# Chain steps moved among the weight units of a two-block transformer kernel

## The chip, the cores and the metric

The kernel runs on one core of a Trainium2 chip. The metric is the device time of one execution in microseconds (us); less is better. TensorE (PE) multiplies matrices, and its weight loads (PEld) are listed apart; VectorE (DVE), ScalarE (ACT) and GpSimd (POOL) work element by element; SyncE (SP) issues the DMAs. Each engine works through its own instructions in a fixed order, and an instruction that waits holds up all that stand behind it on that engine.

## The reference

One sequence of 256 tokens with 1024 features goes through two blocks, all in float32. The first block has two layers; the second block one.

```
# first block, twice:
h = rms_norm(x); z = h @ w_in
cq, ckv, kpe, gq, gk, gv, glr, gr, su, gates = split(z)
o_a = mla_mixer(cq, ckv, kpe)   # low-rank attention: q = norm(cq) @ w_uq, k,v = norm(ckv) @ w_ukv
o_b = gla_mixer(gq, gk, gv)     # gated linear attention in chunks of 64
o_c = s5_mixer(su)              # diagonal state space scan, then a GLU
g = sigmoid(gates)              # three gates of 1024
x = x + (g0*(o_a @ w_br_mla) + g1*(o_b @ w_br_gla) + g2*(o_c @ w_br_s5)) @ w_out
x = x + square(relu(rms_norm(x) @ w_ff1)) @ w_ff2
# second block, once:
h = rms_norm(x); q, k, v, glu_in, z_ga, z_gc = split(h @ w_in_2)
y_attn = dilated_attention(q, k, v)                  # 3 groups of 8 heads of 64
u = a * sigmoid(gate), from glu_in                   # 1024 channels
y_conv = silu(layer_norm(depthwise_conv31(u))) @ w_conv_out
x = x + norm((sigmoid(z_ga)*y_attn + sigmoid(z_gc)*y_conv) @ w_mix_out)
x = x + norm((silu(h2 @ gate) * (h2 @ up)) @ w_ffn_out)   # h2 = rms_norm(x)
```

## The kernel before

**Products.** A float32 product is made of three float32r products: each operand is split into a high part H and a low part L, and H·H, L·H and H·L add up in PSUM. `mm_f` (lines 170 to 172) makes 128 output features by 256 tokens, eight blocks of 128 in the contraction, so 24 matmuls of 256 columns for one unit; `mm_t` (lines 176 to 178) makes 128 tokens by up to 512 features.

**Weight units.** The weights stream through the chip once. A unit is 128 rows by 1024 columns: a DMA on SP brings it into `raw`, ACT rounds it to `wH` (line 161), DVE subtracts to get `wL` (line 162), and 24 matmuls use it. Up to three units are prepared ahead. Behind its matmuls most units have an evacuation: ACT or DVE reads the PSUM tile and writes it to SBUF. The tiles `mm` for these have two buffers, so PE can't begin the third unit before the first is evacuated; the chains use `acc` (five buffers) and `tr` (one).

**Chains.** The attention, state space, linear attention and convolution parts are written as generators, one `yield` at each place where they must wait for another engine. They are the chains: `s` (S5, `s5_run`), `l` (gated linear attention, `gla`), `t` (the row statistics of the latents), `a` and `b` (the two halves of the heads in `mla_attn`); and in the second block `c` (depthwise convolution, `conv_gen`), `h` (heads of the dilated attention, `heads`), `n` (layer norm behind the convolution) and `b` (bias tables).

**Order.** Three strings set the order: `SCHED[0]` and `SCHED[1]` for the two layers and `SCHED2` for the second block. A token with a number is a weight unit (`g1_2` is the third unit of gate 1, `ukv1` the unit that makes keys and values of the second half of the heads, `b2_1` the product of branch 2 with its output weights, `co` the convolution's output, `zc` and `za` gates of the second block, `A` and `G` the two halves of the GLU, `m` the mixing product); a token of one letter is one step of that chain, and `!s` runs chain `s` to its end. The functions are called in this order; a scheduler then orders the instructions of each engine, mostly by that order.

**Lines that the prediction speaks of.** In `mla_kv_evac` ACT squares the keys (`mla_sq`, line 852), DVE and POOL make their norms, DVE writes `mla_kn` (lines 861, 862), and ACT then copies the values to `mla_v` (line 863). In `mla_attn` a step `turn_qk` transposes `mla_qn` and `mla_kn` on PE (line 881), `scores` multiplies them (lines 894, 895), and a later step transposes the probabilities (line 919) and multiplies by the values (line 930). The gates' evacuation is `gt` (line 1116). In S5 one step multiplies by `ET` (line 558), the next runs the scan and writes `s5z` (line 578), the next multiplies by it (lines 587, 591). In the linear attention line 699 multiplies `gq` and `gk`, and lines 739 and 745 make its outputs. In the second block the softmax of a head pair is at lines 1487 and 1491 on ACT, its transposes at line 1500 on PE, copied to `pT` (line 1504); the convolution's layer norm ends with a silu (line 1429), and `cH`, `cL` are its split output for the units `co` (lines 1620, 1621).

Of the kernel before, what the change touches and what calls it, by code (L numbers as in the profile page):

```python
# [13 lines left out]
AF = mybir.ActivationFunctionType  # L14
OP = mybir.AluOpType
# [3 lines left out]
S = 256  # L19
# [48 lines left out]
def f_blocks(w, l, c0, nk, n=1):  # L68
    return [(w, l, k, c0 + P * j, c0 + P * (j + 1)) for j in range(n) for k in range(nk)]
# [201 lines left out]
def residual_raw(k, t, accs, scale, g, dst):  # L271

    nc = k.nc
    with k.tc.high_priority(PRI_N):
        for h in range(2):
# [769 lines left out]
def f_unit(k, plan, st, blocks, evac, nk=8):  # L1045
    def run(H, L):
        ps = k.mm_tile()
        k.mm_f(ps[:, :S], H, L, st.hH, st.hL, nk)
        with k.tc.high_priority(PRI_E):
            evac(ps)  # L1050
    plan.unit(blocks, run)
# [481 lines left out]
def plan_second(k, plan, st):  # L1533
    nc = k.nc
    Q0, K0, V0, A0, G0, ZA, ZC = 0, 1536, 3072, 4608, 5632, 6656, 7680
    st.v2, st.q, st.k, st.u = {}, {}, {}, {}

    def gains(u):
        return [k.pp("gpre")[:, i:i + 1] for i in (2 * u, 2 * u + 1)]
# [14 lines left out]

    def glu_a(i):
        def evac(ps):
            st.ga = k.t1("ga")
            nc.scalar.activation(st.ga, ps[:, :S], AF.Identity, bias=k.pp("bglua")[:, i:i + 1])
        f_unit(k, plan, st, f_blocks("w_in_2", 0, A0 + i * P, 8), evac)

    def glu_gate(i):
        def evac(ps):
            th = k.t1("g2th")
            nc.scalar.activation(th, ps[:, :S], AF.Tanh, scale=0.5, bias=k.pp("bglug")[:, i:i + 1])
            u = k.main.tile([P, 30 + S], F32, tag="u", name=f"u{i}")
            nc.vector.memset(u[:, 0:30], 0.0)
            nc.vector.scalar_tensor_tensor(u[:, 30:30 + S], th, 1.0, st.ga, op0=OP.add, op1=OP.mult)
            st.u[i] = u
        f_unit(k, plan, st, f_blocks("w_in_2", 0, G0 + i * P, 8), evac)

# [18 lines left out]
    za, zc, mm, m1, box = {}, {}, {}, {}, {}  # L1589
# [63 lines left out]
    for tok in SCHED2.split():  # L1653
        name, n = tok.rstrip("0123456789"), tok[len(tok.rstrip("0123456789")):]
# [112 lines left out]
CONV_A = (3, 7, 11, 15, 19, 23, 27)  # L1767
NT = "mtmt"
AT1 = 1
PRI_N = 30  # L1770
PRI_M = 30
AT = 1
SCHED = (
# [8 lines left out]
)  # L1782
SCHED2 = (
# [5 lines left out]
)  # L1789
HOLD = 3  # L1790
RAW_V = 1
# [4 lines left out]
def build_plan(k, tc, ins, out, dbg=None):  # L1796
    plan = make(k, tc, ins, out, dbg)
    k.ins, k.out = ins, out
    sts = [K(), K(), K()]
    plan.do(lambda: first(k, sts[0]))  # L1800
    plan_layer(k, plan, 0, sts[0], sts[1], 3)
    plan_layer(k, plan, 1, sts[1], sts[2], 4)
    plan_second(k, plan, sts[2])
    return plan
# [253 lines left out]
class None_TC:  # L2058
    nc = None
# [38 lines left out]
```

## Time and profile before

| | us |
|---|---|
| median of 3 runs | 1443.59 (1443.32 to 1445.24) |
| the profiled execution | 1446.86 |
| its span, first to last instruction | 1445.1 |
| PE busy | 1403.0 (97%) |
| PE weight loads busy | 1274.8 (88%) |
| DVE busy | 1012.7 (70%) |
| ACT busy | 832.2 (58%) |
| POOL busy | 48.5 (3%) |
| DMA | 243.10 MB, mean 168 GB/s |

All times are one execution's. A stretch is named by its start and end in us from the first instruction. Layer 0 takes about 0 to 530 us, layer 1 to about 950, and the second block the rest; the two layers' feed-forward parts and the one of the second block come at the end of each. "PEclk" is the granted clock of PE as a share of 2.4 GHz, so 0.50 is 1.2 GHz.

### The profile page before, as it was taken

The page shows a single profiled execution, that of the slowest core. Times are in us where ns is not written, and L with a number is a line of the kernel's source. Part 1 is how long each engine was busy: PE and PEld are TensorE (multiplying, and loading weights), DVE is VectorE, ACT ScalarE, POOL GpSimd, SP SyncE. Part 2 cuts the span into 40 slices and gives each one's busy share as a digit, 9 for nine tenths or more (in the row PEclk, how much of TensorE's full clock was granted, in tenths as well). Part 3 has the DMA queues.
Part 4 walks back from the last instruction along what each step waited for, and adds up shares of the span by engine and source line. Part 5 has one row for each costly group of instructions (what it writes and reads, how often), then busy time and mean ns, then how long its engine had stood idle before and what let it go on. Part 6 is the DMA issues. An engine that isn't in the chain of part 4 may idle for free.

```text
span 1445.1 us, 26152 instructions
## 1 busy us (share of the span) xinstructions
PE 1403.0 (97%) x10412; PEld 1274.8 (88%) x10412; DVE 1012.7 (70%) x1860; ACT 832.2 (58%) x1455; POOL 48.5 (3%) x51
## 2 busy tenths in 40 slices
PE   7999999999999999999999999999999999999998
PEld 6989898989889889888998999989888979789997
DVE  6967776689455658676667555579999956765555
ACT  6865475467754555465546444466568574644443
POOL 1000111000000000021000000000000000000000
PEclk9999999999999999999999999999999999999999
DMA  6621444555455552334456555565555435465553
GB/s 221 219 88 62 144 153 140 177 192 189 160 173 187 201 179 78 114 121 173 158 178 227 187 186 189 189 215 190 184 159 164 172 133 198 143 213 190 188 185 109
DMA packets 71058, 243.10 MB, mean 168 GB/s; under 512 B 7864, under 2 KB 11656, under 8 KB 70936
## 3 DMA queue, kind: packets, MB, share of 16 engines
q1 hardware_dynamic: 70936, 241.43, 49.4%
q8 instruction: 81, 1.33, 0.4%
q14 instruction: 41, 0.34, 0.1%
HBM read 237.17 MB, written 4.23 MB: 167 GB/s over the span
## 4 chain that ended last, share of the span: by engine, by line
PE 67%; DVE 11%; ACT 5%; DMA 2%; issue 2%; POOL 2%; DVEq 0%; POOLq 0%; SPq 0%; ACTq 0%
PE mm L170 12%; PE mm L171 12%; PE mm L172 12%; PE acc L176 8%; PE acc L177 8%; PE acc L178 8%; DVE wL L162 3%; DMA raw<-in_wst_dram 2%; DVE cv L1372 2%; POOL rsq L185 2%; ACT wH L161 2%; ACT sp L1487 1%; PE acc L558 1%; ACT sp L1491 1%; PE acc L895 0%
## 5 line engine op out<-in xcount | busy, mean ns | idle before, releaser
L162 DVE TENSOR_TENSOR wL<-raw,wH 128x1024 fp32r<-128x1024 f32 (+1 forms) x410 | 495.8, 1210 | 260.3 <-ACT wH L161 254.7
L161 ACT ACTIVATE wH<-raw 128x1024 fp32r<-128x1024 f32 (+1 forms) x410 | 429.1, 1048 | 388.3 <-PE mm L171 204.5
L170 PE MATMUL mm<-hH,wH 128*128 128x256 f32 x1792 | 515.2, 287 | 5.7 <-ACT gt L1116 4.0
L171 PE MATMUL mm<-hL,wH 128*128 128x256 f32 x1792 | 510.8, 285 | 0.0
L172 PE MATMUL mm<-hH,wL 128*128 128x256 f32 x1792 | 510.7, 285 | 0.0
L170 PEld LDWEIGHTS mm<-hH,wH 128*128 128x128 f32 x1792 | 344.5, 192 | 18.0 <-issue 4.8
L171 PEld LDWEIGHTS mm<-hL,wH 128*128 128x128 f32 x1792 | 344.8, 192 | 4.1 <-issue 0.9
L172 PEld LDWEIGHTS mm<-hH,wL 128*128 128x128 f32 x1792 | 344.8, 192 | 1.0 <-issue 0.6
L176 PE MATMUL acc<-wH,fH 128*128 128x512 f32 x344 | 135.4, 394 | 0.0
L178 PE MATMUL acc<-wH,fL 128*128 128x512 f32 x344 | 134.3, 390 | 0.6 <-DVE fL L162 0.6
L177 PE MATMUL acc<-wL,fH 128*128 128x512 f32 x344 | 134.8, 392 | 0.0
L178 PEld LDWEIGHTS acc<-wH,fL 128*128 128x128 f32 x344 | 64.6, 188 | 15.4 <-DVE fL L162 1.3
L1372 DVE SCALAR_TENSOR_TENSOR cv<-u,ppt,cv 128x256 f32<-128x256 f32 x184 | 77.9, 478 | 0.4
L176 PEld LDWEIGHTS acc<-wH,fH 128*128 128x128 f32 x344 | 64.9, 189 | 11.9 <-ACT fH L161 0.7
L177 PEld LDWEIGHTS acc<-wL,fH 128*128 128x128 f32 x344 | 64.9, 189 | 10.5
L161 ACT ACTIVATE fH<-ffr 128x256 fp32r<-128x256 f32 x56 | 23.4, 418 | 66.8 <-DVE ffr L1275 66.6
L162 DVE TENSOR_TENSOR fL<-ffr,fH 128x256 fp32r<-128x256 f32 x56 | 23.7, 423 | 23.5 <-ACT fH L161 23.5
L178 PE MATMUL acc<-wH,hL 128*128 128x512 f32 x96 | 37.9, 394 | 0.9 <-DVE hL L165 0.8
L176 PE MATMUL acc<-wH,hH 128*128 128x512 f32 x96 | 38.2, 399 | 0.5 <-ACT hH L164 0.4
L177 PE MATMUL acc<-wL,hH 128*128 128x512 f32 x96 | 37.8, 394 | 0.9 <-DVE wL L162 0.9
L177 PE MATMUL acc<-wL,mH 128*128 128x512 f32 x96 | 37.8, 394 | 0.0
L176 PE MATMUL acc<-wH,mH 128*128 128x512 f32 x96 | 37.8, 394 | 0.0
(445 smaller groups left out, 2165.9 us busy)
## 6 DMA issues: line engine op xcount, KB each, us to landing
raw<-in_wst_dram SPq DMA_DIRECT2D x420, 512.0 KB, 3.4
xd<-x SPq DMA_DIRECT2D x6, 512.0 KB, 3.5
x<-xd SPq DMA_DIRECT2D x6, 512.0 KB, 4.6
bias<-bdram SPq DMA_DIRECT2D x8, 384.0 KB, 6.5
gnorm<-in_rows_dram SPq DMA_DIRECT2D x3, 512.0 KB, 5.5
raw<-in_wst_dram SPq DMA_DIRECT2D x4, 384.0 KB, 3.5
x<-in_x_dram SPq DMA_DIRECT2D x4, 256.0 KB, 4.2
x<-in_x_dram SPq DMA_DIRECT2D x2, 512.0 KB, 5.8
```

The lines of the kernel that those rows point to most:

```text
L161: nc.scalar.activation(H, src, AF.Copy)
L162: nc.vector.tensor_sub(L, src, H)
L170: nc.tensor.matmul(ps, H[:, w], aH[:, i, :], start=(i == 0), stop=False)
L171: nc.tensor.matmul(ps, H[:, w], aL[:, i, :], start=False, stop=False)
L172: nc.tensor.matmul(ps, L[:, w], aH[:, i, :], start=False, stop=(i == nk - 1))
L176: nc.tensor.matmul(ps, aH[:, ki, tt], H[:, cols], start=start, stop=False)
L177: nc.tensor.matmul(ps, aH[:, ki, tt], L[:, cols], start=False, stop=False)
L178: k.last_mm = nc.tensor.matmul(ps, aL[:, ki, tt], H[:, cols], start=False, stop=stop)
L185: nc.gpsimd.tensor_tensor(o, m, k.mhalf[:, 0:1].to_broadcast([P, n]), op=OP.pow)
L558: nc.tensor.matmul(ps[:, (4 * c + q) * 64:(4 * c + q + 1) * 64], E[:, c, :], us[:, q, :], start=True, stop=True)
L1372: nc.vector.scalar_tensor_tensor(st.cv[:, ct], u(ct, i), w(ct, i), st.cv[:, ct], op0=OP.mult, op1=OP.add)
L1487: nc.scalar.activation(s[i][:, :, cs], s[i][:, :, cs], AF.Exp, scale=-1.0, bias=mj[:, b:b + 1], accum_out=sm[:, b:b + 1])
```

## The change

The three strings are replaced. In `SCHED[0]` 22 entries stand elsewhere, in `SCHED[1]` 22, in `SCHED2` 46, most by one to six places; the set of tokens is the same. The DMAs of the weights follow the units' order. One storage place, `st.ga`, becomes a dictionary by unit, because `A5` now stands ahead of `A3`, `G3`, `A4` and `G4`. A constant `WARM` is added that nothing on this path reads. The same matmuls and element operations are issued, in another order; ACT has 12 loads of its function table where it had 14. Lines behind 1766 have a number that is one higher after the change.

```diff
-    st.v2, st.q, st.k, st.u = {}, {}, {}, {}
+    st.v2, st.q, st.k, st.u, st.ga = {}, {}, {}, {}, {}
...
-            st.ga = k.t1("ga")
-            nc.scalar.activation(st.ga, ps[:, :S], AF.Identity, bias=k.pp("bglua")[:, i:i + 1])
+            st.ga[i] = k.t1("ga")
+            nc.scalar.activation(st.ga[i], ps[:, :S], AF.Identity, bias=k.pp("bglua")[:, i:i + 1])
...
-            nc.vector.scalar_tensor_tensor(u[:, 30:30 + S], th, 1.0, st.ga, op0=OP.add, op1=OP.mult)
+            nc.vector.scalar_tensor_tensor(u[:, 30:30 + S], th, 1.0, st.ga.pop(i), op0=OP.add, op1=OP.mult)
...
+WARM = (256, 256)
...
-    "g2_3 g2_4 a !s g2_0 g2_1 a a a a a g2_6 a a a glu0 a uq1 glu1 a g2_7 b2_0 g2_5 b2_1 ukv1 b b g0_6 b b b g0_0 "
...
+    "s g2_2 ukv0 s !s g2_3 g2_4 a g2_0 g2_1 a a a a a g2_6 a a a glu0 a uq1 glu1 a ukv1 b2_0 g2_5 b g2_7 "
+    "b2_1 b g0_6 b b g0_0 b2_2 b b b g0_1 g0_4 g0_2 b2_3 b g0_3 !a b !b g0_7 g0_5 ",
```

**Place 1: PE in layer 0, where the second half of the heads begins** (around 223 to 239 us before). The rows are the instructions in PE's order; `hH`, `hL` are the normed input (a gate's unit), `s5oH` the output of S5 (a unit of branch 2). Before:

```order
L171 MATMUL mm<-hL,wH 128x256
L881 MATMUL tr<-cst,mla_qn 96x128 x4
L881 MATMUL acc<-cst,mla_kn 96x128 x4
L172 MATMUL mm<-hH,wL 128x256
L170 MATMUL mm<-s5oH,wH 128x256
```

And after:

```order
L171 MATMUL mm<-hL,wH 128x256
L881 MATMUL tr<-cst,mla_qn 96x128 x4
L881 MATMUL acc<-cst,mla_kn 96x128 x4
L172 MATMUL mm<-hH,wL 128x256
L170 MATMUL mm<-hH,wH 128x256
L171 MATMUL mm<-hL,wH 128x256
L172 MATMUL mm<-hH,wL 128x256
L881 MATMUL tr<-cst,mla_qn 96x128 x4
L170 MATMUL mm<-hH,wH 128x256
L894 MATMUL acc<-mla_T 128x128
L895 MATMUL acc<-mla_T 128x256
```

The last matmul of `ukv1` (line 178) is row 1154 of PE's order before and the transposes at line 881 are row 1202, so 47 matmuls of 256 columns lie between; after the change they are rows 1052 and 1181, with 128 between. Behind the transposes four matmuls now lie ahead of the next pair of line 881, and one more ahead of line 894.

**Place 2: ACT in layer 0, behind `ukv0`** (around 175 to 181 us before). The names are as above; `gt_2` and `gt_4` are two gates' tiles, two evacuations each, and `s5w` at line 625 is a square over all of S5's output. Before:

```order
L161 ACTIVATE wH<-raw 128x1024 x2
L863 ACTIVATE mla_v<-acc,mla_rs 128x256
L852 ACTIVATE mla_sq<-acc 128x256
L625 ACTIVATE s5w<-s5y 128x1024
L1116 ACTIVATE gt_2_2180<-mm,ppt 128x256
L161 ACTIVATE wH<-raw 128x1024
L1116 ACTIVATE gt_4_2306<-mm,ppt 128x256
```

And after:

```order
L1116 ACTIVATE gt_2_2180<-mm,ppt 128x256
L161 ACTIVATE wH<-raw 128x1024
L863 ACTIVATE mla_v<-acc,mla_rs 128x256
L852 ACTIVATE mla_sq<-acc 128x256
L625 ACTIVATE s5w<-s5y 128x1024
L1116 ACTIVATE gt_4_2306<-mm,ppt 128x256
```

The second evacuation of `gt_2` has moved from behind `mla_v`, `mla_sq` and `s5w` to ahead of them; it is `gt_4` that stands behind them now.

**Place 3: ACT in the second block, at the last head pair** (around 1165 to 1182 us before). `z` is a gate's evacuation, `sp` the softmax, `cv` the layer norm's silu. Before:

```order
L1429 ACT_TABLE_LOAD
L1429 ACTIVATE cv<-cv,ppt 128x256
L1487 ACT_TABLE_LOAD
L1487 ACTIVATE sp,asm<-sp,amj 128x3x128
L1487 ACTIVATE sp,asm<-sp,amj 128x3x256
L1586 ACTIVATE z<-mm 128x256
L1487 ACTIVATE sp,asm<-sp,amj 128x3x128
L1491 ACTIVATE sp<-sp,asm 128x3x128
```

And after:

```order
L1487 ACTIVATE sp,asm<-sp,amj 128x3x128
L1487 ACTIVATE sp,asm<-sp,amj 128x3x256
L1586 ACTIVATE z<-mm 128x256
L161 ACTIVATE wH<-raw 128x1024
L1491 ACTIVATE sp<-sp,asm 128x3x128
L1491 ACTIVATE sp<-sp,asm 128x3x256
```

The first silu of the layer norm, which stood between the scores and the softmax with a table load on either side, now comes behind the whole softmax, together with three others and with one load.

## Rows read from the trace of the kernel before

**Rows 1.** The page's first part: busy us, share of the span, instructions, by engine.

```profile
PE 1403.0 (97%) x10412; PEld 1274.8 (88%) x10412; DVE 1012.7 (70%) x1860; ACT 832.2 (58%) x1455; POOL 48.5 (3%) x51
```

**Rows 2.** Windows by stage: start:end, length, busy by engine, PE clock, DMA share, GB/s.

```profile
25.90:172.30 146.40, 141.84 (x1436) 130.60 (x1435) 117.02 (x278) 95.46 (x193) 5.68 (x9) 0.97 0.40 133
172.30:264.30 92.00, 86.07 (x656) 81.88 (x656) 62.82 (x157) 55.45 (x110) 12.49 (x7) 0.96 0.43 144
...
957.90:1149.60 191.70, 188.95 (x1454) 174.97 (x1452) 180.75 (x380) 127.31 (x225) 0.00 (x0) 1.00 0.56 180
1149.60:1192.40 42.80, 39.16 (x311) 34.00 (x310) 24.38 (x51) 32.24 (x56) 0.70 (x1) 1.00 0.38 137
```

**Rows 3.** What PE waits for, 25 to 300 us: us in total, times, longest.

```profile
PE tr L881 <- DVE mla_kn L862: 2.5, 1, 2.5
PE mm L170 <- ACT gt L1116: 2.2, 1, 2.2
PE acc L591 <- DVE s5z L578: 1.5, 2, 1.2
...
PE acc L699 <- DVE gk L677: 0.9, 1, 0.9
```

**Rows 4.** The same, 530 to 700 us.

```profile
PE acc L881 <- DVE mla_kn L862: 2.2, 1, 2.2
PE mm L170 <- ACT gt L1116: 1.8, 1, 1.8
PE tr L881 <- DVE mla_kn L862: 1.2, 1, 1.2
```

**Rows 5.** The same, 950 to 1260 us.

```profile
PE tr L1500 <- ACT sp L1491: 1.4, 2, 1.0
PE tr L1500 <- ACT pT L1504: 1.0, 1, 1.0
```

**Rows 6.** Windows, as rows 2, of the stretches at half clock.

```profile
86.10:92.90 6.80, 6.49 (x29) 6.26 (x30) 6.28 (x12) 0.38 (x1) 0.00 (x0) 0.50 0.66 217
...
181.70:185.10 3.40, 3.40 (x19) 3.33 (x18) 2.50 (x6) 2.06 (x4) 1.19 (x1) 0.50 0.00 0
...
232.90:236.30 3.40, 3.40 (x18) 3.26 (x17) 1.20 (x1) 1.67 (x4) 0.00 (x0) 0.50 0.33 119
...
673.30:676.60 3.30, 3.26 (x16) 3.20 (x17) 2.05 (x3) 1.84 (x3) 0.00 (x0) 0.50 0.12 27
```

**Rows 7.** Timeline of PE around `ukv1`, layer 0: start, length, instruction, [idle before <- releaser].

```profile
223.25 0.28 PE L170 MATMUL mm<-hH,wH 128*128 128x256 f32 x1
...
228.77 0.28 PE L171 MATMUL mm<-hL,wH 128*128 128x256 f32 x1
231.59 0.64 PE L881 MATMUL tr<-cst,mla_qn 128*96 128x128 f32 x4 [2.54 <-DVE mla_kn L862]
```

**Rows 8.** Timeline of ACT behind `ukv0`, layer 0.

```profile
178.35 0.47 ACT L863 ACTIVATE mla_v<-acc,mla_rs 128x256 f32<-128x256 f32 x1 [1.98 <-DVE mla_kn L861]
...
179.93 0.48 ACT L1116 ACTIVATE gt<-mm,ppt 128x256 f32<-128x256 f32 x1
```

**Rows 9.** Timeline behind `ukv1`, layer 1: first PE's instruction, ACT's, PE's.

```profile
659.04 0.28 PE L170 MATMUL mm<-hH,wH 128*128 128x256 f32 x1
...
669.78 0.47 ACT L863 ACTIVATE mla_v<-acc,mla_rs 128x256 f32<-128x256 f32 x1 [2.54 <-DVE mla_kn L861]
670.16 0.47 ACT L1116 ACTIVATE gt<-mm,ppt 128x256 f32<-128x256 f32 x1
...
673.34 0.88 PE L881 MATMUL tr<-cst,mla_qn 128*96 128x128 f32 x3 [1.21 <-DVE mla_kn L862]
```

**Rows 10.** Timeline of PE, 103 to 105 us: small matmuls of two chains in turns.

```profile
103.87 0.65 PE L745 MATMUL acc<-gla_S,gq 64*64 64x128 f32 x6
...
104.69 0.43 PE L745 MATMUL acc<-gla_S,gq 64*64 64x128 f32 x2
```

**Rows 11.** Timeline of ACT at the last head pair, second block.

```profile
1166.93 1.28 ACT L1487 ACT_TABLE_LOAD   x1
```

23 rows, old and new, of tables (SCHED, SCHED2) are left out of this document.

## The prediction

> **What bounds the kernel now.** I read the busy line of the page first. PE is busy 1403.0 of 1445.1 us [rows 1]: it sets the time, it has the same matmuls after the change, and an order can win only from the 42.1 us in which PE stands still and from PE running slowly. So the question is where these are. The windows by stage [rows 2] answer it: 25.9–172.3 has 4.6 us without PE, 172.3–264.3 has 5.9, 957.9–1149.6 has 2.8 and 1149.6–1192.4 has 3.6, some 17 us in these four, and all of them lie where the chains stand among the units. The waits of PE [rows 3 to 5] name the causes: the keys `mla_kn` (2.5 us in layer 0; 2.2 and 1.2 in layer 1), a gate's evacuation `gt` (2.2 and 1.8), S5's `s5z` (1.5), `gk` (0.9), and in the second block the softmax and `pT` (1.4 and 1.0).
>
> A second loss does not show as idle time. In four stretches right behind these waits the granted clock is 0.50, that is 1.2 instead of 2.4 GHz [rows 6]: 232.9–236.3 begins 1.3 us after the wait that ended at 231.59 [rows 7], and 181.7 and 673.3 likewise follow waits of 2.2 us and of 1.8 and 1.2 us. At half clock the work of 3.4 us takes 1.7 at full clock, so each costs about 1.7 us, and 86.1–92.9 about 3.4. These four come to 8.5 us that PE's busy time hides.
>
> The profiled execution is 1446.86 us, 3.3 above the median of 1443.59; I make the sum against the former and subtract it from the latter.
>
> **The change part by part.** My method is the same everywhere: the need is the time from what starts a chain of small operations to its end, read from the trace; the lead is the work that PE has in between, counted in the new order. A matmul of 256 columns takes 0.12 us (46 of them from 223.25 to 228.77 [rows 7]). Where the lead is greater than the need the wait is gone.
>
> *Layer 0, `ukv1`.* The last matmul of `ukv1` ends at 223.25, the keys come at 231.59: need 8.3 us. The lead was 47 matmuls, 5.6 us, hence the wait of 2.54 [rows 7]. After it is 128 matmuls, 15.4 us, so the wait goes. What is late next is inside `turn_qk`: only five matmuls (0.6 us) and one transposing group (0.4) lie ahead of line 894, whose operand ACT copies (two copies of 0.68 by their kind, with the semaphores about 1.2–1.4): 0.4 us of new wait. Line 919 then has 3.7 us against 4.4 that the softmax needs: 0.7 more. Waits −1.4 net; the half clock behind it goes, −1.7.
>
> *Layer 0, `ukv0`.* ACT stood 1.98 us idle at `mla_v`, because DVE had not made `mla_kn`, and the evacuation of `gt` queued behind `mla_v`, a square and S5's large square came at 179.93 [rows 8]; PE waited 2.2 us for it. Now `gt_2` is ahead of `mla_v`. What stands behind `mla_v` instead is `gt_4`, which PE needs two units later: I make its evacuation 9.6 us after `ukv0`, needed at 10.1. The margin of 0.5 is thin. With about 0.8 for lines 894 and 919 again: waits −1.4, clock −1.7.
>
> *Layer 1, `ukv1`.* The same queue: `mla_v` idle 2.54 us, `gt` behind it at 670.16 [rows 9], 1.8 us of wait and then 1.2 for the keys [rows 4]. After the change both evacuations of that gate stand ahead of `mla_v`, and ahead of line 881 lie 120 matmuls and a `values` step, 15.2 us; the keys came 14.3 us after `ukv1` (659.04 to 673.34 [rows 9]). Waits −2.8, clock −1.7. The 2.2 us at the other `mla_kn` of layer 1 [rows 4] stay: the tokens from `uq0` to there are the same.
>
> *Layer 0, S5 and linear attention at 75–93.* Between lines 558 and 591 PE had 37 matmuls and waited 1.2 us of the 1.5, then 0.9 for `gk` [rows 3]. After, some 56 stand there, a lead of 7.9 us with a need of 8.3–8.7 (two `wL` of DVE now stand among S5's operations): 0.4–0.8 us remain. 28 matmuls now separate line 591 from 699. Waits −1.6. Of the 3.4 us that the clock costs here I take 2.5.
>
> *Small ones.* Line 745 ran in turns with S5's transposes at 103–106. Six of its matmuls take 0.65 us, two 0.43 [rows 10], so a run costs 0.32 us beside 0.055 for each; four runs fewer give −1.3. The smaller waits on `goL`, `s5z` and `s5us` in both layers: −0.7.
>
> *Second block.* At the last head pair ACT loses two table loads of 1.28 us [rows 11], the scores stand earlier (12.7 us of PE work ahead of line 1500, of which the softmax needs 9.8), so the 1.4 and most of the 1.0 of [rows 5] go: −2.4, between −0.9 and −3.6, which is the whole idle time of that stretch [rows 2]. In 957.9–1149.6 DVE is busy 180.75 of 191.70 [rows 2], so moving tokens there can give only what DVE allows: 0, between −1 and +1. `A5` ahead of `G3` moves only an ACT evacuation behind PE work: 0.
>
> Sum: waits −1.4 −1.4 −2.8 −1.6 −2.0 −2.4 = −11.6; clock −1.7 −1.7 −1.7 −2.5 = −7.6; together −19.2.
>
> *What this leaves out.* Ninety moved entries also shorten leads elsewhere. I count eight whose lead is within 1 us of the need: three at line 591 in layer 0 and two in layer 1 (6.2–7.9 against 6.4–8.7), two at lines 894 and 919, one at `cH`. The waits of this kind before are 0.9–2.5 us [rows 3, 4]. If half of the eight wait 1 us, and a quarter also brings a half-clock stretch of 1.7, that is 4 + 3.4, about 7. It is the least certain term (0 to 26), and I take 7: −12 in all.
>
> For the clock, the rows show a fall to 0.50 behind waits of 2.2–2.5 us. The Trainium skill, "TensorE: Matmul & The Clock Gate", section "Why this matters for your kernels", advises only against gaps of TensorE longer than any in these rows. By it, the waits would not be the cause of the falls, and removing them would not bring the 7.6 back; the traces speak against it, since three of the four falls come within 1.5 us of such a wait. It is the first rival.
>
> **The rivals.** *The half clock stays or moves.* The new order puts small matmuls together (lines 739, 745 and 778 in layer 0), and the clock could fall there as well. For it: one of the stretches, 86.1–92.9, lies in a cluster of small matmuls as well as behind waits. Against it: three do not. Then −11.6 plus half of the new waits' 7, −6 to −8: about 1436.5.
>
> *The waits move on.* PE reaches the next chained step earlier and waits there for the same producer: at 25.9–172.3 DVE is busy 117.02 of 146.40 [rows 2], and what DVE is late with stays late. Then only the waits behind ACT's queue (2.2 and 1.8) and the second block's go, and new ones eat half of that: −3 to 0, about 1442.5. That the strings change nothing in the engines' order is excluded: the orders of place 1 to 3 differ.
>
> *Slower.* The short leads all turn: at each of the eight a wait of about 1.6 us (the middle of 0.9–2.5) with its 1.7 at half clock, 26 us against the 19.2 gained: +7, about 1451. The deciding point is six of the eight; the first to turn would be `gt_4` in layer 0, with 0.5 us of margin.
>
> **How the numbers follow.** Forecast −12: 1443.59 − 12 = 1431.6. Chances: forecast with −8 to −18, 0.55, and beyond −18, 0.05; half clock stays 0.20; waits move on 0.10; slower 0.10. A measurement of this kernel can tell about 0.2%, 2.9 us, from no change. Faster takes the forecast, what lies beyond it and the first rival, 0.80, less 0.02 for forms of that rival that gain under 2.9: 0.78. The second rival and these 0.02 are same, 0.12; slower 0.10. The range leaves out the slower case, 0.10, and the gains beyond 21 us: 1422 to 1443.
>
> **What would show it.** Right: no half clock at the four places of [rows 6], or shorter; PE's idle time at 30–33 us instead of 42.1; the waits for `gt` and for `mla_kn` of `ukv1` gone from the list; the 2.2 us of `mla_kn` in layer 1 still there; 1149.6–1192.4 shorter by about 2. Wrong: waits of over 1.5 us at lines 591, 894 or 919; a wait for `gt_4`; half clock at lines 739 to 778; or PE's idle time unchanged, with the time gone to other lines.

## The result and the profile after

The changed kernel takes 1426.56 us (median of 4 runs, 1424.88 to 1429.05) against 1443.45 before (4 runs, 1442.18 to 1445.24): 0.9883 of the time before, 95% interval 0.9863 to 0.9904, so 17 us less. The profiled execution took 1429.05 us with a span of 1427.2. The forecast was 1431.6 with a range of 1422 to 1443: right in sign, 5 us short in size. The sum came out better than its terms, as the stretches below show.

The page's busy line after, beside [rows 1]:

```profile
span 1427.2 us, 26151 instructions
PE 1394.9 (98%) x10412; PEld 1269.9 (89%) x10412; DVE 1013.2 (71%) x1860; ACT 827.1 (58%) x1453; POOL 49.9 (3%) x51
```

PE stands still for 32.3 us instead of 42.1, and is busy for 8.1 us less with the same 10412 instructions. So in these two profiled executions about half of the gain is waits, the other half is faster running.

To see where it was won, the program is cut at points where PE has issued equally many H·H products (lines 170 and 176) in both kernels. The windows of before between these points (start:end, length, busy by engine, PE clock, DMA share, GB/s):

```profile
24.88:69.67 44.79, 43.61 (x321) 39.80 (x319) 42.64 (x122) 37.37 (x65) 0.11 (x1) 1.00 0.63 209
69.67:151.68 82.01, 79.06 (x902) 72.87 (x898) 58.74 (x128) 50.56 (x116) 3.70 (x6) 0.94 0.27 90
151.68:262.85 111.17, 104.80 (x868) 99.19 (x865) 78.53 (x188) 63.94 (x125) 14.35 (x8) 0.97 0.42 143
533.79:654.85 121.06, 115.78 (x1244) 108.41 (x1243) 87.65 (x188) 65.11 (x134) 10.56 (x10) 0.99 0.36 118
654.85:947.40 292.55, 288.76 (x1898) 262.95 (x1897) 179.03 (x281) 149.11 (x242) 6.40 (x5) 0.99 0.54 185
1148.21:1261.58 113.37, 108.26 (x741) 94.24 (x739) 74.17 (x131) 72.17 (x123) 3.43 (x5) 1.00 0.45 154
```

The same stretches after:

```profile
25.12:71.79 46.67, 44.33 (x354) 40.41 (x352) 43.62 (x130) 38.29 (x69) 0.11 (x1) 1.00 0.59 198
71.79:145.25 73.46, 71.75 (x854) 67.10 (x851) 58.50 (x120) 48.11 (x110) 3.45 (x5) 1.00 0.29 96
145.25:256.45 111.20, 104.37 (x883) 98.17 (x882) 78.33 (x188) 64.14 (x127) 15.28 (x9) 0.98 0.42 147
526.97:649.04 122.07, 118.04 (x1244) 110.76 (x1243) 87.21 (x188) 65.31 (x134) 11.02 (x10) 0.96 0.35 117
649.04:936.67 287.63, 286.99 (x1899) 261.66 (x1897) 179.07 (x281) 148.54 (x242) 6.39 (x5) 1.00 0.54 188
1136.43:1243.72 107.29, 106.11 (x740) 93.77 (x739) 74.73 (x132) 69.09 (x121) 3.74 (x5) 1.00 0.46 165
```

Subtract the lengths, stretch by stretch. The opening: +1.88 us. Layer 0's S5 and linear attention: −8.55. Layer 0's attention, where I had put two of my terms: +0.03. Layer 1 up to `ukv1`: +1.01. Layer 1 behind `ukv1`: −4.92. The end of the second block: −6.08. (Not shown: 947 to 1148 is 1.05 shorter.) The cut goes by H·H products alone, so small matmuls can change sides: the opening has 33 PE instructions more after the change, S5's stretch 48 fewer and the attention 15 more. Opening and S5's stretch together are 6.67 us shorter, and PE's idle time in the two is the same (4.13 and 4.05 us). In the stretch that stayed equal, PE's idle time did not change either: 6.37 before, 6.83 after. The waits of PE after, 25 to 300 us, say why:

```profile
PE acc L591 <- DVE s5z L578: 3.1, 2, 2.4
PE tr L881 <- DVE mla_kn L862: 2.8, 2, 2.1
PE mm L170 <- ACT su L1082: 1.5, 1, 1.5
PE mm L171 <- DVE s5oL L165: 1.0, 1, 1.0
```

The 2.2 us for `gt` of [rows 3] are gone, but S5's wait in this stretch has grown from 0.3 to 2.4, the keys of `ukv1` still cost 2.1 instead of 2.5, and those of `ukv0` cost 0.7 that were not there. The wait for `s5oL` is old; before it was

```profile
PE mm L171 <- DVE s5oL L165: 0.9, 1, 0.9
```

In layer 1 the two waits behind `ukv1` [rows 4] are gone but for 0.6, and the one that I had left is there:

```profile
PE acc L881 <- DVE mla_kn L862: 2.2, 1, 2.2
PE acc L176 <- DVE mla_qn L837: 1.1, 1, 1.1
PE mm L170 <- ACT gt L1116: 0.6, 1, 0.6
```

The stretches at half clock after, as windows (before there were seven such places, four of them in [rows 6]; either run has one more at its very end, where PE has no work left):

```profile
172.40:175.80 3.40, 3.40 (x55) 3.23 (x44) 3.09 (x7) 0.00 (x0) 1.91 (x1) 0.50 0.42 143
541.00:544.40 3.40, 3.40 (x14) 3.22 (x15) 3.40 (x8) 0.44 (x1) 0.00 (x0) 0.50 0.35 82
582.00:585.40 3.40, 3.40 (x73) 3.00 (x71) 1.56 (x4) 0.14 (x2) 1.60 (x1) 0.50 0.44 147
619.50:622.90 3.40, 2.77 (x13) 2.78 (x14) 2.40 (x6) 1.87 (x10) 0.72 (x2) 0.50 0.46 131
```

The first follows a wait of 2.4 us and the last begins inside one of 2.2; the two in the middle follow no wait of PE over 0.6 us.

### The profile page after: what moved, and what is told of

Its sections match the earlier page's. It is cut to its first block, busy times and chain, and to the rows that moved or that the text cites. A ratio compares the mean times of both kernels' runs of the same rounds, so it can differ in the third digit from the quotient of the medians.

```text
span 1427.2 us, 26151 instructions
## 1 busy us (share of the span) xinstructions
PE 1394.9 (98%) x10412; PEld 1269.9 (89%) x10412; DVE 1013.2 (71%) x1860; ACT 827.1 (58%) x1453; POOL 49.9 (3%) x51
## 4 chain that ended last, share of the span: by engine, by line
PE 77%; DVE 10%; ACT 6%; DMA 2%; issue 2%; POOL 2%; SPq 0%; DVEq 0%; POOLq 0%; ACTq 0%
PE mm L170 13%; PE mm L171 13%; PE mm L172 13%; PE acc L176 9%; PE acc L177 9%; PE acc L178 9%; DVE wL L162 4%; DVE cv L1372 2%; DMA raw<-in_wst_dram 2%; ACT wH L161 2%; POOL rsq L185 1%; PE acc L558 1%; PE acc L591 1%; PE acc L1512 1%; PE acc L587 1%
## 5 line engine op out<-in xcount | busy, mean ns | idle before, releaser
L176 PEld LDWEIGHTS acc<-wH,fH 128*128 128x128 f32 x344 | 64.9, 189 | 11.3
L178 PE MATMUL acc<-wH,mL 128*128 128x512 f32 x96 | 37.8, 397 | 0.0
```

Source lines behind the costliest of these rows:

```text
L176: nc.tensor.matmul(ps, aH[:, ki, tt], H[:, cols], start=start, stop=False)
L178: k.last_mm = nc.tensor.matmul(ps, aL[:, ki, tt], H[:, cols], start=False, stop=stop)
```

## A measure that takes the clock apart

Each run lists its span and its mean granted clock. Span times clock is an estimate of the time that the run would take at full clock; the rest is put down to half clock. Runs of one kernel differ by up to 12 us (before: 1437.94 to 1449.7), and most of it is this rest. So each kernel is told by both means, with the standard error, in us (the clock is listed to 0.001, 0.7 us either way in one run):

| kernel | runs | mean time | at full clock | lost to half clock |
|---|---|---|---|---|
| before | 45 | 1444.95 | 1430.9 ± 0.2 | 12.2 ± 0.5 |
| after | 4 | 1426.76 | 1419.6 ± 0.5 | 5.4 ± 1.2 |
| e1 string of layer 0 alone | 12 | 1440.73 | 1428.7 ± 0.5 | 10.2 ± 0.9 |
| e2 string of layer 1 alone | 6 | 1437.47 | 1427.6 ± 0.6 | 8.1 ± 0.8 |
| e3 string of the second block alone | 6 | 1436.04 | 1424.7 ± 0.6 | 9.6 ± 1.6 |
| e4 its tail alone | 6 | 1439.31 | 1425.1 ± 0.6 | 12.5 ± 0.5 |
| e5 after, `ukv1` late | 5 | 1427.72 | 1418.5 ± 0.5 | 7.4 ± 1.3 |
| e7 after, two table loads back | 6 | 1430.37 | 1421.2 ± 0.6 | 7.4 ± 0.9 |
| e8 after, scan early | 4 | 1428.74 | 1419.1 ± 0.8 | 7.9 ± 1.5 |
| e9 after, lead in layer 1 | 4 | 1426.66 | 1418.8 ± 0.7 | 6.1 ± 0.4 |
| e10 e5 and e9 together | 5 | 1426.43 | 1418.4 ± 0.5 | 6.3 ± 0.4 |
| e11 before, gates ahead in layer 1 | 12 | 1446.66 | 1430.6 ± 0.5 | 14.3 ± 0.9 |
| e12 e10, and more lead in layer 0 | 6 | 1426.40 | 1418.5 ± 0.7 | 6.2 ± 0.6 |

By this measure the change is worth 11.3 us at full clock and 6.9 by the clock. The measure has two limits. First, it gives the clock too much: among the 45 runs of before, one that lost 1 us more to half clock took only 0.7 us longer, for half clock also falls where PE has nothing to do (3.9 us at the end of the profile before, 2.1 after). Read so, the clock's share is nearer 5 us. Second, the 45 runs are three groups (17 beside e1 to e4, 11 beside e5, e7, e8 and e9, 17 beside e10 to e12), with means of 1431.6, 1430.1 and 1430.8 at full clock, further apart than their errors; the four runs of the changed kernel belong to none of them. So a difference of under 1.5 us between kernels of different groups is not shown, whatever its error below says.

## Experiments: which string gains

Each of e1 to e3 takes one of the three strings from the changed kernel and leaves the other two:

```diff
 SCHED = (
-    <layer 0, before>
+    <layer 0, after>
     <layer 1, before>
```

> Only the string of layer 0 is the new one. Theory A, the sum of the prediction (each wait weighed with the need read from the trace before): -12.0 us before what new waits take back, about -8 after. Theory B, the two traces compared at equal counts of matmuls: -6.4 us at the end of layer 0, all of it gained at 70 to 152 us, mostly as clock, and nothing at 152 to 263, where waits at lines 591 and 881 stand again. Under B the time is about 1437 and these two waits are in the profile; under A they are under 1 us.

Measured: median 1439.85 us, 0.997 of before (0.9956 to 0.9984). At full clock −2.2 ± 0.5, by the clock −2.0. That is below both theories' numbers. The waits are those of theory B, in the profile of e1:

```profile
PE acc L591 <- DVE s5z L578: 3.1, 2, 2.5
PE tr L881 <- DVE mla_kn L862: 2.8, 2, 2.1
```

So they belong to the order of layer 0, and the 12 us that I had counted there were not to be had.

> Only the string of layer 1 is the new one. Theory A: -4.8 us (-4.5 behind ukv1, -0.3 elsewhere). Theory B, from the traces at equal counts of matmuls: -4.9 behind ukv1 and +1.0 ahead of it, where two stretches at half clock are new, so -3.9. If those two stretches belong to the order, they are seen again; if they fall by chance, the run may be -7.

Measured: median 1437.12 us, ratio 0.9949 (0.9936 to 0.9962). At full clock −3.4 ± 0.7, by the clock −4.1, together 7.5, near the 7 us that were expected if the two new half-clock stretches fall by chance. The profiles say the same: the one at 541 us was not seen again, and the one at 582 was (587 us), but it stands as well in four of the five profiles with the old order of layer 1 up to there (585 us in e1, 591 in e3, 590 in e4 and e11). Neither belongs to the new order.

> Only the string of the second block is the new one. Theory A: -2.4 us, all of it at the last head pair. Theory B, from the traces at equal counts of matmuls: -7.1 us, of which -1.0 ahead of the last conv step, -6.1 behind it.

Measured: median 1437.14 us, ratio 0.9939 (0.992 to 0.9958). At full clock −6.3 ± 0.6: theory B.

The fourth leaves the second block's string as before up to the last conv step:

```diff
-... !c za1 n h h n h h zc1 h n h h zc2 zc3 n h h h zc5 h zc7 h zc4 zc0 h n h h h h n !n co4 ...
+... !c za1 h n h h h zc1 n h zc3 h h h zc2 h n h zc5 zc7 n h n h zc4 zc0 h h n h h h co0 !n h ...
```

> As before, but the string of the second block is the new one from the token !c on (za1, zc, n, h, co, ao, m). Theory B: -6.1 us if the tail alone makes its gain; -2.4 if the sum of the prediction is right and the rest comes from the earlier steps of the heads, which this kernel leaves as before.

Measured: median 1439.3 us, ratio 0.9961 (0.9947 to 0.9976). At full clock −5.9 ± 0.6, nearly all of e3's 6.3: the tail makes the second block's gain alone. The three strings add up to −11.9 at full clock against −11.3 for all together. Against the 17 runs of before taken beside them alone, e1 to e4 come to −2.9, −4.1, −7.0 and −6.6, and the three strings to −13.9 ± 1.1: the order of the parts stays, and the sum is known to about 2 us.

## Experiments: what the waits hang on

The first of these puts `ukv1` of layer 0 back to its late place in the changed kernel:

```diff
-... uq1 glu1 a ukv1 b2_0 g2_5 b g2_7 b2_1 b g0_6 b b g0_0 b2_2 b b b g0_1 ...
+... uq1 glu1 a g2_7 b2_0 g2_5 b2_1 ukv1 b b g0_6 b b b g0_0 b2_2 b b g0_1 ...
```

> The changed kernel with the units from glu1 on in layer 0 in the old order, so that ukv1 stands late again. Theory A, the prediction's: the early place was worth 3.1 us, so this is about 1429.7. Theory B, from the trace after: with ukv1 early, the squares of its keys (line 852) stand on ACT behind weight roundings (line 161) that wait for PE, the keys need 19 us instead of 8.3 and PE waits 2.11 us all the same, and 0.97 for s5oL; so the late place costs nothing, 1426.6 within 1.5, with a wait of about 1.8 us at line 881 (lead 6.5 us, need 8.3).

Measured: median 1428.95 us, ratio 0.9889 (0.9871 to 0.9907). At full clock −1.1 ± 0.7 against the changed kernel, so the waits that theory A counted (1.4 of its 3.1) are out; by the clock +2.0 ± 1.8, which alone could not exclude the other 1.7. The profile settles it for one execution: the attention's stretch, with one half-clock stretch in it as in the changed kernel, takes 110.94 us where that took 111.20, and the keys' wait is 1.4 instead of 2.1:

```profile
144.05:254.99 110.94, 104.32 (x884) 98.13 (x882) 78.34 (x188) 64.20 (x127) 13.47 (x9) 0.98 0.44 148
PE tr L881 <- DVE mla_kn L862: 2.1, 2, 1.4
```

The early place is worth nothing here. Why is seen on ACT behind the early `ukv1`, whose last matmul starts at 205.44 (timeline of ACT after; start, length, instruction, [idle before <- releaser]):

```profile
212.77 1.06 ACT L161 ACTIVATE wH<-raw 128x1024 fp32r<-128x1024 f32 x1 [1.34 <-PE mm L171]
213.74 0.46 ACT L1116 ACTIVATE gt<-mm,ppt 128x256 f32<-128x256 f32 x1
214.09 0.38 ACT L852 ACTIVATE mla_sq<-acc 128x256 f32<-128x256 f32 x1
```

The first operation on the keys comes 8.6 us after their last product began (214.09 less 205.44). It stands on ACT behind roundings of weights (line 161) that wait until PE has used up an older unit. On PE:

```profile
205.44 0.39 PE L178 MATMUL acc<-wH,ckvL 128*128 128x512 f32 x1
224.88 0.64 PE L881 MATMUL tr<-cst,mla_qn 128*96 128x128 f32 x4 [2.11 <-DVE mla_kn L862]
```

19.4 us from the start of the last product to the transposes, where before it was 8.6 (231.59 [rows 7] less the start of the last product, 223.03). From the start of the last product PE had 17.3 us of work and small waits (222.77 less 205.44), 11.3 more than the 6.0 of before, and the need grew by 10.9. That ACT's order is the cause is read from the trace; no run moves the squares alone.

The next shows the same from the other end. In the kernel before, one edit in layer 1 brings the gate's evacuations ahead of the keys' second square and of `mla_v` on ACT:

```diff
-... ukv1 a g1_1 g1_0 a a b1_0 b ...
+... ukv1 g1_1 g1_0 b1_0 a a a b ...
```

> The kernel before with one edit in layer 1: the two gate units behind ukv1 and the branch unit b1_0 stand ahead of the last steps of the first half of the heads. On ACT both evacuations of the gate now stand ahead of the second square of the keys and of mla_v; on PE 11.2 us of work lie ahead of line 881, where 10.2 us and a wait of 1.8 lay. If the need is a constant 14.3 us, the wait for gt goes and one of 3.1 for the keys stands in its place: 0. If the need itself shrinks because nothing waits in ACT's queue, both waits go or stay under 0.5: -2.5, and -4 with the half clock.

Measured: median 1446.45 us, ratio 1.001 (0.9993 to 1.0026). At full clock −0.4 ± 0.6: nothing. Waits of PE in e11, 530 to 700 us:

```profile
PE tr L881 <- DVE mla_kn L862: 3.5, 1, 3.5
PE acc L881 <- DVE mla_kn L862: 2.2, 1, 2.2
```

The 1.8 us for `gt` of [rows 4] are gone and the keys' wait has grown from 1.2 to 3.5. The need, from the end of `ukv1` to the transposes, is in e11

```profile
658.14 0.28 PE L170 MATMUL mm<-hH,wH 128*128 128x256 f32 x1
673.19 1.09 PE L881 MATMUL tr<-cst,mla_qn 128*96 128x128 f32 x4 [3.47 <-DVE mla_kn L862]
```

15.05 us, where before it was 14.3: nearly constant, and no shorter for the freed queue. So the queue at `gt` had only held part of a wait that the keys would have caused anyway. The changed kernel has the same gates ahead of `mla_v` and 15.2 us of forecast lead at this place, and there the keys' wait goes and 0.6 is left of the one for `gt` (e2: −4.0 us over 655 to 740). The longer lead without the gates' move was not tried.

Three kernels then try to win the waits that the change left. In e8, layer 0 issues S5's last scan ahead of the queries:

```diff
-... b1_2 s s uq0 s b1_3 s g2_2 ukv0 s !s g2_3 g2_4 a ...
+... b1_2 s s s uq0 b1_3 g2_2 s ukv0 s !s g2_3 g2_4 a ...
```

> The changed kernel, but in layer 0 the last scan step of S5 stands ahead of uq0 instead of behind it, and the matmul step ahead of ukv0. In the trace after, PE waits 2.44 us at line 591, since the scan (line 571) stands on DVE behind both query tiles of uq0. If a lead counted with DVE's own order is the right measure (11 us of PE work against 6.4 to 8.7), this wait goes, and with it the half clock at 172: -2.4 to -4 against the changed kernel, 1423. If the waits only move on, 0.

Measured: median 1428.2 us, ratio 0.989 (0.9871 to 0.9909). At full clock −0.5 ± 0.9. Waits in e8, 25 to 300 us:

```profile
PE tr L881 <- DVE mla_kn L862: 6.4, 2, 4.2
PE acc L591 <- DVE s5z L578: 0.6, 1, 0.6
```

S5's 2.4 us are gone; the keys of `ukv0`, 0.7 in the changed kernel, now cost 4.2. The wait moved from one consumer of DVE's work to the next.

In e9, layer 1 gets more work ahead of the first half's keys:

```diff
-... g2_2 g2_3 l l uq0 ukv0 l l a !s glu0 a !l a g2_4 a glu1 a g2_7 a g2_5 a g2_6 ...
+... g2_2 l l uq0 g2_3 ukv0 l l g2_4 !s glu0 !l glu1 g2_7 a a a a a g2_5 a a g2_6 ...
```

> The changed kernel, but in layer 1 one gate unit stands between uq0 and ukv0 and one more unit between ukv0 and the first transposes of the heads: 11.5 us of PE work ahead of line 881 where 8.6 stood and 10.9 were needed. If the lead decides, the waits of 2.22 us (mla_kn) and 1.1 us (mla_qn) go: -2.5 to -5 against the changed kernel, 1422 to 1424. If they move on, to line 764 or 919, 0 to -1.

Measured: median 1426.48 us, ratio 0.9876 (0.9857 to 0.9894). At full clock −0.8 ± 0.9. Waits in e9, 530 to 700 us:

```profile
PE tr L764 <- DVE gla_og L759: 2.1, 1, 2.1
PE acc L176 <- DVE mla_qn L837: 1.1, 1, 1.1
```

The keys' 2.2 us are gone, as the lead says; the output of the linear attention, 0.7 in the changed kernel, now costs 2.1, and the queries' 1.1 stayed in spite of a unit put between. The time by the median is that of the changed kernel.

> The changed kernel with both edits of the runs e5 (ukv1 late in layer 0) and e9 (more lead in layer 1). Work at full clock, that is span times mean clock, was 1418.5 and 1418.8 for these two and 1419.6 for the changed kernel; if the two edits add up this gives about 1417.7, and with 6 us lost at half clock a time of 1425.5, within the noise of the changed kernel's 1426.6.

Measured: median 1426.55 us, ratio 0.9878 (0.9858 to 0.9897). At full clock 1418.4, 1.2 ± 0.7 under the changed kernel.

The last adds to e10 the scan of e8 and a lead taken from e8's own trace:

```diff
-... b1_2 s s uq0 s b1_3 s g2_2 ukv0 s !s g2_3 g2_4 a g2_0 g2_1 a a a a a g2_6 a ...
+... b1_2 s s s uq0 b1_3 s ukv0 g2_2 s !s g2_3 g2_4 g2_0 a g2_1 a a a a a g2_6 a ...
```

> As e10, and in layer 0 the scan step early as in e8, with ukv0 one unit earlier and the first transposes one unit later: 11.5 us of PE work ahead of line 881 instead of the 7.2 of e8, where the need was 11.4. If leads against needs taken from e8's own trace decide, the waits of 2.44 at line 591 (of the changed kernel) and 4.19 at line 881 (of e8) both fall under 1 us: -2 us against e10 at full clock. If the need grows again with the order, 0.

Measured: median 1426.49 us, ratio 0.9878 (0.9857 to 0.9898). At full clock the same as e10. With `ukv0` three us earlier its keys came hardly earlier: PE is through with the rest at 174.0 and gets them 2.35 us late, at 176.4, where e8 had 176.7. So this need is not counted from `ukv0`. The trace of e12 has the second square of these keys again behind a rounding that waits for PE:

```profile
168.21 1.06 ACT L161 ACTIVATE wH<-raw 128x1024 fp32r<-128x1024 f32 x1 [1.18 <-PE mm L171]
169.17 0.46 ACT L1116 ACTIVATE gt<-mm,ppt 128x256 f32<-128x256 f32 x1
169.53 0.38 ACT L852 ACTIVATE mla_sq<-acc 128x256 f32<-128x256 f32 x1
```

In e8 the same square starts at 169.40. Whether it or DVE's work ahead of the keys sets the moment, no run tells apart. None of e8 to e12 is clearly better than the changed kernel.

## Experiment: the table loads in the second block

The changed kernel with a tiny silu ahead of the last head pair's softmax:

```diff
         sm = k.sm(2, "asm")
+        sp == 3 and i == 0 and nc.scalar.activation(k.sm(2, "extra"), mj, AF.Silu)
```

> The changed kernel with a tiny silu on ACT ahead of the last head pair's softmax, which brings back the two table loads of 1.28 us (and puts one silu of the layer norm ahead of the softmax's last scaling). If the two loads were what the tail of the second block saved, this is 2 to 3 us slower than the changed kernel, about 1429. If the earlier scores (12.7 us ahead of line 1500 against 9.8 needed) were it, 2.6 us more on ACT fits in, and it is 0 to 0.7 us.

Measured: median 1429.09 us, ratio 0.9901 (0.988 to 0.9923). At full clock +1.6 ± 0.8 against the changed kernel. Waits of PE in e7, 950 to 1250 us, with one of 1.7 at the last head pair that is 0.4 in the changed kernel:

```profile
PE acc L1512 <- ACT pT L1504: 1.7, 1, 1.7
```

The 1.6 ± 0.8 lies between the two numbers that were to be told apart; against e5, e8 and e9, measured beside it, it is 2.4 ± 0.7. The wait of 1.7 shows that the loads did not fit in whole behind the earlier scores. At that size they carry a quarter to two fifths of the tail's 5.9 us. That can be too little: in e7 the first load ran where ACT had to wait anyway (from 1145.12; behind it ACT still waits 1.84 us for `amj`), while before both loads stood at 1165 to 1168 with no idle time of ACT around them. A load holds ACT for 1.28 us [rows 11], and the exp behind it began 1.30 us after the load's start. The Trainium skill, "ScalarE: Activation LUTs", section "What ACT_TABLE_LOAD costs", adds a drain and gives about 2.66 us for a switch. The trace shows no such drain at this place. Two switches by that figure would be an estimated 5.3 us; 1.6 to 2.4 was measured, at a place with some slack. Of the rest of the tail, 3.9 us are PE's idle time (5.11 to 1.18 in the windows above, the loads' part among it) and 2.1 are PE busy for less time with the same matmuls. How the 2.1 come about was not tried apart.

## Why the prediction held, step by step

**The bound.** Right but for a small part: of the 17.9 us between the two profiles, 9.8 are PE's idle time and 6.8 its half-clock stretches; the last 1.3 is PE busy for less time at full clock, which the prediction allowed only for line 745.

**Layer 1, `ukv1`: −4.5.** Right: −4.92 in the windows, and the wait that was to stay, 2.2 us, stayed. The reason was put too broadly. The prediction gave ACT's queue a share; e11 shows that freeing the queue alone is worth nothing, so the longer lead was needed.

**Layer 0, `ukv1` and `ukv0`: −3.1 each.** Wrong: +0.03 together. The step that failed is the need taken as a constant from the trace before. It holds where the chain's operations stand in the same company on ACT and DVE (layer 1: 14.3 and 15.05). In layer 0 the unit moved away from its company, and its keys' operations came to stand behind weight roundings that wait for PE: 8.6 us became 19.4. Place 1 of the change, on PE, does not show this; ACT's order at the same place does, and I did not read it there. The last scan of S5, on DVE behind both query tiles, was missed in the same way and cost 2.4.

**Layer 0, 75 to 93: −1.6, −2.5 by the clock, −1.3 for the runs of line 745.** Right in sum only. The stretch 69.67 to 151.68 is 8.55 shorter: 1.2 idle, 5.1 by the clock (6.8 and 3.4 us at half clock before, none after), 2.2 of busy time. But with the opening, to which small matmuls moved and where the wait for `su` grew from 0.5 to 1.5, it is 6.67, and nothing of that is idle time. And a part of the clock's share is luck: the stretch at 86 us, for which 2.5 was counted, came in two of the five profiles with the old string of layer 0 (before and e2). Where it did not come, in e3 and e4, this stretch of the old order is 2.85 us shorter than in the profile of before.

**Second block: −2.4, at most −3.6.** Mis-sized: −6.08 in the windows, −5.9 in e4. The bound was the idle time of 1149.6 to 1192.4 alone. Busy time can shrink as well, the stretch that gains is longer, and I left the wait for `cL` at line 1621 (0.95 us) standing, which went.

**New waits: 7.** Near in size, but by luck. Of the eight short leads one turned: line 591 in layer 0, 2.4 us where it had been 0.3. Lines 894 and 919, `cH` and line 591 in layer 1 show no wait of note. Not on the list came 0.7 for the keys of `ukv0` and 1.0 more for `su`. That is about 4 us, and 1.7 for the half clock at 172. The sum from which the 7 were taken, 19.2, already had 6.2 of layer 0 that never came.

**The clock: −7.6.** Right in size as far as the measure goes (−6.9 ± 1.3 over the runs, which is an upper value; the six kernels made from the changed one lost 6.1 to 7.9 us, so that its 5.4 in four runs may be low), half right in its cause. The same wait at the same place brings half clock in one execution and not in the next. In the thirteen profiles of before, after and all experiments, waits of PE of 2 us and more were followed by a stretch at 0.50, or had one begin inside them, in 22 of 38 cases (36 of these waits are of 2.1 to 2.6 us, 20 of the 36 with a fall), though half clock takes only some 24 us of a run of before: `gt` and the keys in layer 0 of the old order (2.2 and 2.5 us) four of five each, S5's 2.4 of the new order five of six, but the keys' 2.1 of the new order never in four and the keys' 2.2 of layer 1 four of ten. The pair of 1.8 and 1.2 us behind `ukv1` in layer 1 [rows 4] went with one in all four profiles that have it, and with none in the eight that wait 0.6 us or less there. And stretches at 0.50 come without such a wait, at 109 to 126 and 541 to 598 us, among small matmuls of S5 and linear attention or close behind them; so the first rival was right that half clock lies there too, in both orders. The Trainium skill, "TensorE: Matmul & The Clock Gate", section "Why this matters for your kernels", advises only against gaps of TensorE longer than the 36; as the only cause of a fall it would have given back nothing. These rows speak against that: the runs lost 12.2 us before and 5.4 after.

**The rivals.** The waits that move on were given 0.10; in layer 0's attention, and in e8, e9 and e12, just this happened. The slower case did not come near. Of the signs of being wrong that the prediction named, one came: the wait of 2.4 us at line 591. Of the signs of being right, PE's idle time (32.3 us), half clock gone from its four places (in this profile), the wait that stays in layer 1 and the missing `gt` came; the keys of `ukv1` in layer 0 did not leave the list.

That the forecast ended 5 us from the measured time is in part luck: the discount of 7 happened to be near the 6.2 of layer 0's attention that never came. Most of what it fell short by is the 3.7 us more in the second block.

## What to carry to other kernels

Weigh a moved unit by lead and need, but read the need in the new order: on the in-order engines that make the awaited data, look what stands ahead of the first of their operations, above all work that itself waits for the consumer. A wait taken away at one consumer is a gain only if the next consumer of the same producer has slack; look there before counting it. Where runs list span and mean clock, compare their product as well, within runs taken side by side, since it is steadier than the time: over the 45 runs of before it spread by 1.4 us (standard deviation) where the time spread by 2.4.

## What the runs showed of the hardware that was not expected

The granted clock falls to half in short stretches that differ between executions of one kernel: in runs of the kernel before, the mean clock lay between 0.987 and 0.996, and the time followed it (1449.26 us at 0.987, 1437.94 at 0.996). What half clock costs one run of this kernel is so a matter of chance; only the mean, by the measure above 12.2 us before and 5.4 after, belongs to an order.
